# The recurrence of a four-mixer network: kk transposed by 128-token blocks, state sums on the diagonal blocks, 16x16 inverses one block to a lane, and a new order

## The chip, the core and the metric

The kernel is one program on one core of a Trainium2 chip. Five engines run side by side, each in its own order: TensorE (PE; the loading of its stationary operand is listed as PEld), VectorE (DVE), ScalarE (ACT), GpSimd (POOL) and SyncE (SP); the last two mostly start transfers. The metric is device microseconds (us) of one execution; lower is better.

## The reference, cut to what matters

Four mixers, each followed by a feed-forward block, on 512 tokens of width 1024 in float32. The change lies in the first mixer, a gated recurrence over tokens with 16 heads of width 64:

```
def step(state, inp):
    r_t, d_t, k_t, v_t, kk_t, a_t = inp
    sa = jnp.einsum('bhvk,bhk->bhv', state, kk_t)
    state = (state * d_t[:, :, None, :]
             - sa[..., None] * (kk_t * a_t)[:, :, None, :]
             + v_t[..., None] * k_t[:, :, None, :])
    return state, jnp.einsum('bhvk,bhk->bhv', state, r_t)
```

The other mixers (windowed attention, a gated chunk mixer, gated linear attention) and the feed-forward blocks are not touched, but the order of their instructions is.

## The kernel before

**A program that orders itself.** The code first records every operation (line 253 is where each of them is issued, so nearly all rows of the profile carry L253 and are told apart by tile and shape). `Program.run` then picks, engine by engine, which recorded operation goes next, from prices written in the code and from a turn: the operation's own number, shifted by the table `TURNS`, whose entries (first, last, shift) move a range of operations forward or back. When TensorE would have nothing to do for long, or too little in the last window, it is given products of the identity with itself into a spare bank (line 520, `products`): these are the fills.

**The recurrence in chunks.** The 16 heads are worked in four groups of four (two pairs of heads, i = 0, 1, each pair in 128 rows, the second head h in the upper 64). The 512 tokens are four blocks of 128 (b), each of two chunks of 64 (c). For a group, `ahead(n)` runs these, in this order:

- `rwkv_prepare`: decays, keys and the scaled vectors. Tile `qk` of a pair holds for each block four pieces of 64 columns, r, kk, kk, r (outer pieces r, inner pieces kk); `kb` holds the keys likewise.
- `rwkv_products`: for each 128 columns and each head one product of `kb` with `qk`, masked on VectorE into tile `pr` (odd groups) or `pa` (even groups). It holds for each unit (block, pair, head) the triangular matrices that couple the tokens of a chunk.
- `rwkv_inverse`: the 64x64 triangular matrices are inverted, beginning with their 16x16 diagonal blocks. These are gathered into a tile of 128x512 (`et`) whose second half of each 32 columns is zero, transposed in 32x32 squares on VectorE, and inverted by substitution in 15 steps (one product and one sum each, two blocks to a lane); another transpose, a mask (`mt`), and two levels of 64x64 products on TensorE build the whole inverse (`iv`).
- `rwkv_direct`: kk is transposed on TensorE (128 columns of `qk` at a time, so that each transpose carries one piece of r that nobody uses) and multiplied with the inverse; the result goes back into the inner pieces of `qk`.

Then `rwkv_chain` goes through the eight chunks one after another. A step takes the state `st` (128x256, for each pair two 64x64 blocks on the diagonal of a 128x128 square, the rest kept at zero), adds its product with `qk` to the chunk's values (bank `x`), copies that to `vu`, sums `tok` transposed times `vu` onto the old state in bank `pb`, and scales the sum by the chunk's decay (`pend`) into the next state. `rwkv_out` normalizes and gates the result.

While the chain of group n runs, `ahead(n + 1)` is worked beside it; the first group is worked beside the product that makes the values, and the last chain beside the output product over the first three groups (`rwkv_out_proj`, tiles `et` and `rk`). So VectorE, ScalarE and TensorE each mix instructions of a chain with those of the next group.

## Time and profile before

| what | value |
|---|---|
| median of 3 runs | 2467.82 us (2465.43 to 2470.07) |
| the profiled execution | 2470.02 us |
| its span, first to last instruction | 2468.3 us |
| TensorE clock granted, mean | 0.997 of full speed |

On a profile's rows: a group of instructions is written as line, engine, operation, output <- inputs (tile names without numbers), shapes, xcount, then busy us and mean ns of one, then the idle time just before them and who ended it. A matmul of float32 leaves two records or more, a transpose one. The busy us of a group count overlapping instructions once; the mean of one is its own duration, so on TensorE the mean is longer than the spacing. A line of a window gives, for a stretch from:to, its length, the busy us of each engine with its instructions in brackets, the granted clock, the share of the transfer engines and GB/s.

### The profile page before, as it was taken

What the parts mean: (1) busy time and instruction counts of PE and PEld (TensorE: products, weight loads), DVE (VectorE), ACT (ScalarE), POOL (GpSimd) and SP (SyncE); (2) the same over time, 40 slices, a digit from 0 to 9 for tenths busy, and PEclk for the clock granted to TensorE, in tenths of its full rate; (3) what the DMA queues carried; (4) which work ended last, traced back from release to release, by engine and by line L of the source; (5) the groups of instructions that cost most, each with busy time, mean ns of one, the idle gap of its engine ahead of it and who ended that gap; (6) DMA issues with size and microseconds to landing.
All of it is one profiled execution on the core that took longest, in us unless ns stands there. A gap on an engine that the chain in (4) does not pass through costs nothing.

```text
span 2468.3 us, 37524 instructions
## 1 busy us (share of the span) xinstructions
PE 2411.1 (98%) x14166; PEld 1995.9 (81%) x14166; DVE 1930.5 (78%) x3051; ACT 1389.3 (56%) x2267; POOL 400.2 (16%) x456
## 2 busy tenths in 40 slices
PE   9999999999999999999999999999999999999998
PEld 7677789987888768988887788887878788888886
DVE  8686995786779885777789886976868978886868
ACT  4545544664646476656466544854546756755555
POOL 0000000111112241121111300211111221212111
PEclk9999999999999999999999999999999999999999
DMA  5220002589898234898988835889897775989885
GB/s 170 71 71 10 11 11 81 137 226 215 208 221 187 75 107 103 192 238 192 233 189 202 218 99 153 183 201 216 200 225 182 187 181 124 187 214 227 216 211 125
DMA packets 128629, 400.85 MB, mean 162 GB/s; under 512 B 14384, under 2 KB 21040, under 8 KB 128448
## 3 DMA queue, kind: packets, MB, share of 16 engines
q0 software_dynamic: 50688, 171.99, 39.2%
q1 hardware_dynamic: 77760, 226.47, 27.2%
q8 instruction: 111, 1.82, 0.3%
q14 instruction: 70, 0.57, 0.1%
HBM read 393.95 MB, written 2.10 MB: 160 GB/s over the span
## 4 chain that ended last, share of the span: by engine, by line
PE 71%; DMA 9%; DVE 9%; ACT 5%; issue 4%; POOL 1%; SPq 0%; DVEq 0%; POOLq 0%; ACTq 0%
PE ps L253 71%; DMA wraw<-ffn_w_a 3%; DMA wraw<-ffn_w_b 2%; DVE wlo L253 2%; ACT slot L253 2%; DVE slot L253 2%; DMA wraw<-ffn_o_a 2%; ACT whi L253 1%; DVE h L253 1%; POOL wraw L253 1%; DVE et L253 1%; DMA wraw<-sg_w_v 1%; DVE mt L253 0%; DMA wraw<-gla_w_qk 0%; POOL slot L253 0%
## 5 line engine op out<-in xcount | busy, mean ns | idle before, releaser
L253 PE MATMUL ps<-whi,slot 128*128 128x512 f32 (+1 forms) x4960 | 1509.7, 385 | 13.7 <-DVE slot L253 7.4
L253 PEld LDWEIGHTS ps<-whi,slot 128*128 128x128 f32 x4960 | 923.4, 188 | 186.2 <-DVE slot L253 14.7
L253 ACT CAST whi<-wraw 128x1024 fp32r<-128x1024 f32 (+2 forms) x680 | 673.8, 997 | 619.5 <-PE ps L253 426.6
L253 DVE TENSOR_TENSOR wlo<-wraw,whi 128x1024 fp32r<-128x1024 f32 (+2 forms) x680 | 783.7, 1161 | 237.9 <-ACT whi L253 233.8
L253 PE MATMUL ps<-wlo,slot 128*128 128x512 f32 (+1 forms) x2480 | 932.7, 383 | 4.1 <-DVE wlo L253 4.1
L253 PEld LDWEIGHTS ps<-wlo,slot 128*128 128x128 f32 x2480 | 466.8, 188 | 85.7 <-DVE wlo L253 7.9
L253 PE MATMUL ps<-slot,whi 128*128 128x512 f32 (+3 forms) x976 | 276.1, 366 | 1.8 <-ACT slot L253 0.9
L253 DVE TENSOR_TENSOR slot<-ps,slot 128x512 f32<-128x512 f32 (+2 forms) x269 | 159.0, 607 | 79.7 <-PE ps L253 70.6
L253 PEld LDWEIGHTS ps<-slot,whi 128*128 128x128 f32 (+2 forms) x976 | 170.4, 184 | 40.4 <-issue 4.5
L253 POOL DMA_DIRECT2D wraw<-ffn_w_a x128 | 111.0, 879 | 483.2 <-DVE wlo L253 339.4
L253 DVE TENSOR_TENSOR h<-h,ps 128x512 f32<-128x512 f32 x240 | 159.0, 684 | 26.6 <-PE ps L253 24.3
L253 DVE TENSOR_TENSOR slot<-left,slot 128x512 fp32r<-128x512 f32 x250 | 160.2, 662 | 23.5 <-ACT slot L253 15.4
L253 PE MATMUL ps<-slot,wlo 128*128 128x512 f32 (+3 forms) x488 | 176.5, 366 | 0.0
L253 ACT CAST slot<-left 128x512 fp32r<-128x512 f32 (+1 forms) x250 | 143.4, 601 | 29.0 <-PE ps L253 18.0
L253 ACT COPY slot<-ps 128x512 f32<-128x512 f32 (+2 forms) x154 | 85.3, 566 | 72.4 <-PE ps L253 66.0
L253 PEld LDWEIGHTS ps<-slot,wlo 128*128 128x128 f32 (+2 forms) x488 | 89.5, 184 | 18.4 <-issue 3.7
L253 POOL DMA_DIRECT2D wraw<-ffn_o_a x64 | 55.9, 873 | 297.3 <-DVE wlo L253 210.5
L253 POOL DMA_DIRECT2D wraw<-ffn_w_b x64 | 55.1, 867 | 300.2 <-DVE wlo L253 99.4
L253 PE MATMUL ps<-ident,slot 128*128 128x128 f32 (+2 forms) x672 | 88.8, 265 | 6.6 <-DVE slot L253 6.4
L253 PEld LDWEIGHTS ps<-ident,slot 128*128 128x128 f32 (+2 forms) x672 | 68.8, 140 | 31.1 <-DVE slot L253 10.6
L253 DVE TENSOR_TENSOR slot<-slot 128x512 fp32r<-128x512 f32 (+7 forms) x131 | 77.2, 611 | 12.1 <-DMA slot<-slot 7.2
L253 ACT COPY left<-ps 128x512 f32<-128x512 f32 x100 | 51.0, 555 | 44.1 <-PE ps L253 44.0
(281 smaller groups left out, 2242.0 us busy)
## 6 DMA issues: line engine op xcount, KB each, us to landing
wraw<-ffn_w_a SPq DMA_DIRECT2D x128, 512.0 KB, 6.4
wraw<-ffn_w_a POOLq DMA_DIRECT2D x128, 512.0 KB, 7.9
wraw<-ffn_o_a SPq DMA_DIRECT2D x64, 512.0 KB, 5.1
wraw<-ffn_o_a POOLq DMA_DIRECT2D x64, 512.0 KB, 7.1
wraw<-ffn_w_b SPq DMA_DIRECT2D x64, 384.0 KB, 4.0
wraw<-ffn_w_b POOLq DMA_DIRECT2D x64, 384.0 KB, 6.6
wraw<-ffn_o_b SPq DMA_DIRECT2D x16, 512.0 KB, 3.9
wraw<-ffn_o_b POOLq DMA_DIRECT2D x16, 512.0 KB, 7.3
```

The source lines that it names most:

```text
L253: op = self.add(eng.name, lambda: getattr(eng.target, what)(*map(real, args), **{k: real(a) for k, a in kw.items()}), *self.price(eng.name ...
```

## The change

- **kk by blocks of 128 tokens.** The two inner pieces of `qk` change places (chunk 0's kk stands at piece 2, chunk 1's at piece 1), so the two middle pieces of a block, 128 columns, are just the two chunks' kk. One transpose takes them both: four for a pair where there were eight, and one copy where there were two. Writing the pieces in the new places takes two products and two small copies on VectorE for one of each. In `rwkv_products` the right operand picks its two pieces with a step.
- **16x16 inverses, a block to a lane.** ScalarE gathers the diagonal blocks into the full 128x512 tile (no zeros); after the transpose one select takes for each lane the half that is its own; the substitution goes two rows at a time on 256 columns, with a one-column update in between; ScalarE copies the result into both halves before the second transpose, and the mask is applied in two parts. The mask's last column is inverted (`odd` becomes `even`), and the identity that is loaded for it is 256 wide.
- **State sums on the diagonal blocks.** In `rwkv_chain` the product of `tok` and `vu` is made for each head alone, 64x64 outputs into the two halves of the rows, and from the second chunk on the scaling is one product over the whole 128x256 tile.
- **`TURNS`** is written anew: finer ranges, other shifts, for all stages.

```diff
 TURNS = (
-    (0, 192, -3283), (192, 384, -2134), (384, 412, -1837), (412, 464, -482), (464, 492, -1382), (536, 588, -2292), (616, 644, 25), (696, 724, -1506),
...
-    (16911, 17104, -1), (17104, 17297, -15), (17297, 17490, 81), (17490, 17683, -5), (17683, 17876, 295), (17876, 18069, 278), (18069, 18262, 2577),
+    (0, 96, -1837), (96, 192, -1135), (192, 288, -902), (288, 384, -841), (384, 412, 180), (464, 492, 721), (492, 508, 1201), (536, 588, 116),
...
+    (17847, 17948, 1984), (17948, 18048, 2039), (18048, 18149, 3494), (18149, 18250, 9031),
 )
...
+            mid = lambda t, c: t.rearrange("p (b x c) -> p b x c", b=NB, x=4)[:, :, 2 - c, :]
...
-            nc.vector.tensor_mul(inner(qk)[:, :, :, 1:], nat(kk)[:, :, :, 1:], nat(e)[:, :, :, :C - 1])
-            nc.vector.tensor_copy(inner(qk)[:, :, :, 0], nat(kk)[:, :, :, 0])
+            for c in range(2):
+                nc.vector.tensor_mul(mid(qk, c)[:, :, 1:], nat(kk)[:, :, c, 1:], nat(e)[:, :, c, :C - 1])
+                nc.vector.tensor_copy(mid(qk, c)[:, :, 0], nat(kk)[:, :, c, 0])
...
-                    nc.tensor.matmul(ps[h][:, c * P:(c + 1) * P], sb['kb'][i][q, t], sb['qk'][i][q, t], start=c == 0, stop=True, skip_group_check=True)
+                    qk = sb['qk'][i].rearrange("p (b x c) -> p b x c", b=NB, x=4)[q, hf * 2 + c // 2, c % 2:c % 2 + 3:2, :]
+                    nc.tensor.matmul(ps[h][:, c * P:(c + 1) * P], sb['kb'][i][q, t], qk, start=c == 0, stop=True, skip_group_check=True)
...
-        nc.gpsimd.memset(zx4[:, :, 1, :], 0.0)
+        zx, n, tt = [self.part("et") for _ in range(3)]
+        nc.sync.dma_start(tt[:, :256], self.d['rw_eye'])
...
-            nc.vector.scalar_tensor_tensor(zx4[r, :, 0, :], z3[r, o + 16:o + 32, :], mk['odd'][r], z3[r, o:o + 16, :],
-                                           op0=ALU.mult, op1=ALU.add)
+            nc.scalar.copy(zx[r].rearrange("p (t x u) -> p x t u", t=16, x=2), zc[r, o:o + 32, :].rearrange("p (x t) u -> p x t u", x=2))
         nc.vector.transpose(n, zx)
-        for i in range(1, 16):
-            w = tmp[:, :2 * i * i].rearrange("p (b j m) -> p b j m", b=2, j=i)
-            nc.vector.tensor_mul(w, n4[:, i, :, :i].unsqueeze(2).to_broadcast([P, 2, i, i]), t4[:, :, :i, :i])
-            nc.vector.tensor_reduce(t4[:, :, :i, i], w, axis=AX.X, op=ALU.add)
-        tx = self.part("et")
-        nc.vector.transpose(tx, tt)
+        nc.vector.scalar_tensor_tensor(n3, nb[:, :, 0, :], mk['even'], nb[:, :, 1, :], op0=ALU.mult, op1=ALU.add)
+        for i in range(0, 16, 2):
+            if i:
+                w = n[:, :2 * i * i].rearrange("p (c j m) -> p c j m", c=2, j=i)
+                nc.vector.tensor_mul(w, n3[:, i:i + 2, :i].unsqueeze(2).to_broadcast([P, 2, i, i]), t3[:, :i, :i].unsqueeze(1).to_broadcast([P, 2, i, i]))
+                nc.vector.tensor_reduce(t3[:, :i, i:i + 2].rearrange("p j c -> p c j"), w, axis=AX.X, op=ALU.add)
+            nc.vector.scalar_tensor_tensor(t3[:, :i + 1, i + 1], t3[:, :i + 1, i], n3[:, i + 1, i:i + 1], t3[:, :i + 1, i + 1], op0=ALU.mult, op1=ALU.add)
+        nc.scalar.copy(zx.rearrange("p (j b i) -> p j b i", j=16, b=2), t3.unsqueeze(2).to_broadcast([P, 16, 2, 16]))
+        nc.vector.transpose(n, zx)
...
-            src = tu[:, k * 8:k * 8 + 8, :].unsqueeze(2).to_broadcast([P, 8, 4, 16])
-            nc.vector.tensor_mul(t0.rearrange("p (u b j) -> p u b j", u=8, b=4), src, b16)
+            for g in range(2):
+                nc.vector.tensor_mul(t0.rearrange("p (u g x j) -> p g u x j", u=8, g=2, x=2)[:, g], tu[:, k * 8:k * 8 + 8], b16[:, g].unsqueeze(1).to_broadcast([P, 8, 2, 16]))
...
+            kt, tp = self.part("mt"), self.bank()
+            for b in range(NB):
+                nc.tensor.transpose(tp[:, b * P:(b + 1) * P], sb['qk'][i][:, b * 256 + 64:b * 256 + 192], self.ident)
+            nc.scalar.copy(kt, tp)
             for bb in range(2):
-                kt, tp = self.part("mt"), self.bank()
-                for j in range(4):
-                    t = (bb * 4 + j) * P
-                    nc.tensor.transpose(tp[:, j * P:(j + 1) * P], sb['qk'][i][:, t:t + P], self.ident)
-                nc.scalar.copy(kt, tp)
...
-                    for i in range(G):
-                        mm(pb[:, col(i)], tok[:, col(c * 2 + i)], vu[:, col(i)], start=st is None and i == 0, stop=True)
+                    for i, h in heads:
+                        mm(pb[h * 64:(h + 1) * 64, hc(i, h)], tok[:, c * W:(c + 1) * W][:, hc(i, h)], vu[:, hc(i, h)], start=st is None and i == 0, stop=True)
...
-                    for h in range(2):
-                        pend = sb['pend'][h * 64:(h + 1) * 64, :, 2 * b + c].unsqueeze(2).to_broadcast([64, G, 64])
-                        nc.vector.tensor_mul(block(ns, h), block(pb, h), pend)
+                    if st is None:
...
+                    else:
+                        two = lambda t: t.rearrange("p (g c) -> p g c", g=G)
+                        nc.vector.tensor_mul(two(ns), two(pb), sb['pend'][:, :, 2 * b + c].unsqueeze(2).to_broadcast([P, G, P]))
```

More of the change, by code (lines that the diff above doesn't have):

```diff
@@ L1115, in rwkv @@
         m = lambda j: mk[:, j * 64:(j + 1) * 64]
-        self.mk = dict(prod=mk[:, :2 * P], low=(m(4), m(5)), b16=m(6), odd=mk[:, 7 * 64:])
+        self.mk = dict(prod=mk[:, :2 * P], low=(m(4), m(5)), b16=m(6), even=mk[:, 7 * 64:])
         ka1 = cp.tile([P, KT], F32, name="ka1")
@@ L1292, in rwkv_inverse @@
-        tx = self.part("et")
-        nc.vector.transpose(tx, tt)
-        tu = tx.rearrange("p (j u) -> p u j", j=16)
-        b16 = mk['b16'].rearrange("p (b j) -> p b j", b=4).unsqueeze(1).to_broadcast([P, 8, 4, 16])
+        nb = n.rearrange("p (t b m) -> p t b m", t=16, b=2)
+        n3, t3 = [t[:, :256].rearrange("p (a b) -> p a b", a=16) for t in (zx, tt)]
+        nc.vector.scalar_tensor_tensor(n3, nb[:, :, 0, :], mk['even'], nb[:, :, 1, :], op0=ALU.mult, op1=ALU.add)
[5 more added lines that the diff above has]
+            nc.vector.scalar_tensor_tensor(t3[:, :i + 1, i + 1], t3[:, :i + 1, i], n3[:, i + 1, i:i + 1], t3[:, :i + 1, i + 1], op0=ALU.mult, op1=ALU.add)
@@ L1912, in consts @@
     low = [(s6 // (2 * m) == c // (2 * m)) & (s6 % (2 * m) >= m) & (c % (2 * m) < m) for m in (16, 32)]
-    masks = [even, odd] + low + [s6 // 16 == c // 16, (s % 32 >= 16)]
+    masks = [even, odd] + low + [s6 // 16 == c // 16, (s % 32 < 16)]
     masks = np.concatenate([m.astype(np.float32) for m in masks], axis=1)
-    f = np.arange(S)
-    eye = np.broadcast_to((f // 32 == f % 16).astype(np.float32), (P, S)).copy()
+    f = np.arange(256)
+    eye = np.broadcast_to((f // 16 == f % 16).astype(np.float32), (P, 256)).copy()
     return {'rw_masks': masks, 'rw_eye': eye, 'rope_freq': freq}
```

14 lines of the change are left out of this document (7 added, 7 removed), and 40 rows, old and new, of the table TURNS.

## The prediction, made before the changed kernel had run

> **What bounds the kernel now.** The profiled execution took 2470.0 us, 1.7 more than its span, and lies 2.2 above the median of the runs. I read the page first, then busy time in stretches, then the chain of waits in the recurrence, then single instructions.
>
> ```profile
> span 2468.3 us, 37524 instructions
> PE 2411.1 (98%) x14166; PEld 1995.9 (81%) x14166; DVE 1930.5 (78%) x3051; ACT 1389.3 (56%) x2267; POOL 400.2 (16%) x456
> ```
>
> TensorE has work nearly everywhere, so what leaves TensorE shortens the run, and what leaves VectorE does so only where TensorE waits for it. Busy time by stage, with everything first and the filling products (line 520) second:
>
> ```profile
> core 0: us, PE busy (x) PEld busy (x) DVE busy (x) ACT busy (x) POOL busy (x), PEclk, DMA share, GB/s
> 175.00:250.00 75.00, 72.75 (x912) 56.08 (x911) 52.20 (x118) 37.84 (x73) 2.92 (x6) 1.00 0.03 9
> 250.00:395.00 145.00, 138.36 (x2287) 115.16 (x2288) 123.46 (x289) 70.06 (x154) 7.80 (x13) 1.00 0.08 24
> 395.00:460.00 65.00, 64.98 (x618) 61.23 (x610) 37.16 (x99) 25.34 (x53) 1.91 (x2) 1.00 0.39 120
> ```
> ```profile
> 250.00:395.00 145.00, 6.20 (x44) 5.38 (x44) 1.00 0.08 24
> 395.00:460.00 65.00, 4.56 (x38) 4.48 (x38) 1.00 0.39 120
> ```
>
> Stage 1 (175 to 250: value product, first group, its chain) and stage 3 (395 to 460: last chain beside the output product) are full of TensorE. In stage 2 TensorE idles 145 − 138.4 = 6.6 us and fills 6.2: a slack of 12.8 in which it waits for others. Which others, the chain of waits for stage 2 says, by line and then in pieces:
>
> ```profile
> by line: PE ps L253 45.5%; DVE et L253 12.5%; DVE mt L253 6.7%; DVE out L253 3.5%; issue 3.3%; DVE pa L253 3.0%; DVE h L253 2.5%; DVE pr L253 2.5%; DVE qk L253 1.8%; DVE iv L253 1.8%; ACT L253 1.8%; DVE st L253 1.7%; DVE gmean L253 1.4%; AC
> ```
> ```profile
> 285.88 0.65 DVE et L253
> 286.54 0.65 DVE et L253
> 287.21 0.66 DVE et L253
> 287.88 0.68 DVE et L253
> ```
> ```profile
> PE ps L253 <- DVE st L253: 2.4, 3, 1.1
> ```
>
> TensorE carries 45.5% of 145, 66 us. The listed VectorE items sum to 37.4%; with the cut-off tail I take 40%, 58 us (estimate). The four pieces are the gather of a group's diagonal blocks, standing on the path. VectorE, busy 123.5 of 145, is the second bound, although the longest of TensorE's own waits in stage 2 (last line: the state, us in total, times, longest) is small.
>
> **Part 1, kk transposed at once.** Per group 16 transposes become 8 and four 128x512 copies on ScalarE become two.
>
> ```profile
> L253 PE MATMUL ps<-ident,qk 128*128 128x128 f32 x64 | 11.0, 284 | 0.0
> L253 ACT COPY tok<-ps 128x512 f32<-128x512 f32 x16 | 9.5, 591 | 5.7 <-PE ps L253 5.4
> L253 PE MATMUL ps<-qk 64*128 64x128 f32 x128 | 10.0, 281 | 0.7 <-DVE qk L253 0.7
> L253 DVE TENSOR_TENSOR qk<-et 128x504 f32<-128x504 f32 x4 | 2.7, 678 | 0.4 <-ACT et L253 0.4
> L253 DVE COPY qk<-et 128x8 f32<-128x8 f32 x4 | 0.7, 167 | 0.0
> ```
>
> A transpose takes 11.0 / 64 = 0.17 us of TensorE; 32 fewer are 5.5 us, a quarter (1.4) in stage 1 and the rest (4.1) in stage 2. ScalarE loses 8 x 0.59 = 4.7. The products' right operand now skips one 64-column block; counts and widths are the same. I take zero: the odd groups' products are the third line, 10.0 us, so all four groups' take 20, and a tenth more would be 2. On VectorE one product and one small copy (last lines) become two of each for each of a group's two pairs of heads; at 0.42 for a product of half the width (a row of part 2), 2 x 0.42 − 0.68 + 0.17 = 0.33, 0.7 per group.
>
> **Part 2, the state sum on its diagonal blocks.** A step's two full products (four records) become four 128x64 ones on 64 columns (eight records), into alternate halves of the output partitions. Nearest pieces, one after another, start us and length first:
>
> ```profile
> 353.44 0.68 PE L253 MATMUL ps<-wu,iv 64*64 64x64 f32 x16
> 354.05 0.71 PE L253 MATMUL ps<-st,ident 128*128 128x128 f32 x4
> 355.67 0.71 PE L253 MATMUL ps<-vu,tok 128*128 128x128 f32 x4
> 356.31 0.68 PE L253 MATMUL ps<-vu,pa 128*64 128x64 f32 x8
> 356.92 0.33 PE L253 MATMUL ps<-ident,qk 128*128 128x128 f32 x1
> ```
>
> Start to start the old form takes 356.31 − 355.67 = 0.64 us. Eight records of the new shape, all into one half, take 356.92 − 356.31 = 0.61 (vu,pa); alternating halves, 16 smaller records take 354.05 − 353.44 = 0.61, so eight take 0.31 (wu,iv). The new cost lies between 0.31 and 0.61; I take 0.34, near the alternating row, as the outputs alternate: 0.30 saved a step (0.03 at worst). The Trainium skill, in TensorEngine Tiling (Array Packing), section Key Properties, says that tiles of the array run independently but a change of tiling mode drains it. The alternating row agrees with the first half; by that the step saves the 0.30, and without it 0.03.
>
> ```profile
> L253 PE MATMUL ps<-vu,tok 128*128 128x128 f32 x112 | 19.2, 294 | 1.4 <-ACT vu L253 0.9
> 175.00:250.00 75.00, 4.69 (x28) 1.00 0.03 9
> 250.00:395.00 145.00, 10.43 (x62) 1.00 0.08 24
> 395.00:460.00 65.00, 4.14 (x24) 1.00 0.39 120
> ```
>
> 112 records are 28 steps; by stage (second to fourth line) 7, 15 and 6: 2.1, 4.5 and 1.8 us. The state itself:
>
> ```profile
> L253 DVE TENSOR_TENSOR st<-ps,pend 64x128 f32<-64x128 f32 x56 | 16.1, 287 | 16.0 <-PE ps L253 15.4
> L253 DVE TENSOR_TENSOR h<-ps,h 128x256 f32<-128x256 f32 x16 | 6.2, 420 | 3.4 <-PE ps L253 3.3
> ```
>
> Two half products (16.1 / 28 = 0.58) become one 128x256 at 0.42, except in each chain's first step: 24 x 0.16 = 3.8, some 13 of them (2.1) in stage 2. Off the diagonal the sum stays zero, since the state there was cleared and is only multiplied.
>
> **Part 3, the 16x16 inverses.** Four 32-partition gathers move from VectorE to four 32x512 copies on ScalarE, one 128x256 select follows the transpose, 15 pairs of product and sum become seven pairs on the even sizes with eight one-column updates, and ScalarE widens the result (128x512) before the second transpose.
>
> ```profile
> L253 DVE SCALAR_TENSOR_TENSOR et<-pr,mk 32x256 f32<-32x256 f32 x8 | 5.2, 655 | 0.1
> L253 DVE TENSOR_TENSOR et<-et 128x2 f32<-128x2 f32 (+14 forms) x15 | 4.9, 328 | 0.3
> L253 DVE TENSOR_REDUCE et<-et 128x2 f32<-128x2 f32 (+14 forms) x15 | 4.8, 323 | 0.3
> L253 DVE TENSOR_TENSOR et<-et 128x8 f32<-128x8 f32 x3 | 0.5, 168 | 0.0
> L253 DVE TENSOR_TENSOR et<-et 128x392 f32<-128x392 f32 x3 | 1.7, 554 | 0.0
> L253 DVE SCALAR_TENSOR_TENSOR grs<-rs_t,grs 128x8 f32<-128x8 f32 x24 | 4.3, 180 | 0.4
> L253 ACT COPY et<-kkrs 128x512 f32<-128x512 f32 x6 | 3.7, 628 | 0.0
> ```
>
> From 8 to 392 elements a product grows 386 ns: 1.0 ns an element over 0.16 us. The seven kept sizes (2 x i x i for i = 2 to 14) hold 1120 elements: 7 x 0.16 + 1.12 = 2.2 us, and as much for the sums. So 4.9 + 4.8 − 4.4 = 5.3 goes, with 4 x 0.655 = 2.6; eight updates at 0.18 (1.4) and a select at 0.42 come. Splitting the two 128x512 masks into four of half width adds two starts of 0.16 (0.3). With the 0.7 of part 1 VectorE is relieved of 7.9 − 2.8 = 5.1 us a group. In stage 2 fall the second half of group 1's inverse and all of groups 2 and 3: 2.4 x 5.1 = 12.2. ScalarE gains 5 x 0.63 − 2 x 0.59 = 2.0 a group, hidden in its 75 idle us of stage 2; without that cover 8 us in all. No row has the strided gather on ScalarE: at best 0.63 each, at worst twice that, as the 32x256 gather on VectorE costs 655 against 420 for a plain 256-wide one. I take 0.7: 2.8 in series, against 2.6 now. The transposes now wait for ScalarE twice, and behind the first of them stand state products and masks of the running chain; a copy that is late by one other copy costs 0.6, eight times 4.8 at worst, and the order puts other VectorE work ahead. The constant's load on SP's queue halves and is done early; the fill of zeros on GpSimd goes.
>
> **Part 4, places.** All turns are new, up to the last stage. After 460 TensorE waits thus:
>
> ```profile
> 460.00:2468.30 2008.30, 1964.48 (x9542) 1633.59 (x9540) 1585.04 (x2306) 1166.25 (x1850) 384.89 (x422) 1.00 0.77 184
> PE ps L253 <- DVE slot L253: 20.1, 15, 3.5
> 600.00:625.00 25.00, 21.50 (x91) 17.30 (x90) 12.58 (x14) 11.60 (x15) 2.59 (x3) 0.93 0.78 189
> ```
>
> Of 43.8 idle us, 20.1 in 15 waits stand behind VectorE. The work there is unchanged, so I take zero, bounded by half of that row, 10 us, either way.
>
> **Sum.** Stage 1: 1.4 + 2.1 = 3.5. Stage 2 by capacity: 4.1 + 4.5 = 8.6, and half of the slack of 12.8, 15.0; by the chain: 58 x (12.2 + 2.1) / 123.5 + 66 x 8.6 / 132.2 (busy less fills) = 6.7 + 4.3 = 11.0. I take 13.0, the middle. Stage 3: 1.8. Together 18.3: 2470.0 becomes 2451.7, and the median 2467.8 becomes **2449.5**.
>
> **Rivals.** *A, VectorE hides:* only TensorE's work counts, the slack stays, and part of it is filled again: 5.5 + 8.4 = 13.9 less two waits of the longest kind after 460 (3.5 each), 2461. For it: TensorE named only 2.4 us of waits for the state. Against it: the chain stands on VectorE for 58 us. *B, more:* all slack of stage 2 goes (3.5 + 21.4 + 1.8 = 26.7) and the places win up to 10: 2431 to 2441. For it: 20.1 us in 15 waits behind VectorE are there to be moved. *C, slower:* in the feed-forward stages a weight load or its adding load is put later in SP's or GpSimd's queue, and TensorE waits as at 600 to 625: 3.5 idle and 0.07 x 25 of clock, 5.3 a gap. Four gaps cancel the forecast; from five it is slower by more than noise, 6 give 2467.8 − 18.3 + 31.8 = 2481. For it: the transfers' share there is 0.78; against: TensorE's long waits there name VectorE. *D, the clock:* with less TensorE work the recurrence is granted less; at a mean of 0.75 over the 132.2 − 8.6 = 123.6 us of work left in stage 2 it costs 41, 2490. In every stage's row the clock stands at 1.00, even with 6.6 idle. The Trainium skill, in TensorE: Matmul & The Clock Gate, Part 1, has the clock halved after a window of some 3.4 us without matmuls; the row of 600 to 625 agrees, and none of the recurrence comes near. *E, it does not do what it says:* the new products do not overlap (0.03 x 28 = 0.8) and the gathers take 1.26 each, 2.4 a group later, 7 over three groups, which eats VectorE's relief: 2467.8 − 6.3 + 3 = 2465.
>
> **Chances.** Forecast 0.48 (2444 to 2456), A 0.20, B 0.18, C 0.07, D 0.03, E 0.04. The range 2433 to 2464 holds forecast, A and two thirds of B; left out are the rest of B, C, D and most of E, under 0.2. No change means within 0.2% (4.9 us), what a measurement of this kernel can tell: faster 0.48 + 0.18 + 0.18 of A = 0.84, same 0.02 + 0.04 = 0.06, slower 0.10.
>
> **What would show it.** Part 1: 32 fewer transposes and eight fewer 128x512 copies. Part 2: tok records 128x64, twice as many, under 0.4 us a step, and 24 state products of 128x256 near 0.42. Part 3: seven pairs a group, gathers on ScalarE near 0.7. Sum: the output product's start comes 15 to 17 us earlier, VectorE's busy time falls by about 4 x 5.1 + 3.8 = 24, and after 460 idle stays near 44. I am wrong if stage 2 keeps its length with more fill, or if the time after the recurrence moves by more than 10.

## The result, and the profile after

The changed kernel takes 2469.52 us (median of 12 executions, 2462.29 to 2475.57), the kernel before in the same comparison 2469.55 (12, 2462.62 to 2473.57): a ratio of 1.0004, 95% interval 0.9991 to 1.0016. Nothing was gained where 18.3 us were forecast. The profiled execution took 2467.0. Page of the changed kernel, span and busy time by engine:

```profile
span 2465.3 us, 37624 instructions
PE 2399.4 (97%) x14222; PEld 1985.7 (81%) x14222; DVE 1909.0 (77%) x3007; ACT 1408.0 (57%) x2282; POOL 404.4 (16%) x452
```

The work did leave its engines: TensorE 11.7 us less, VectorE 21.5 less (24 were forecast), ScalarE 18.7 more. So the question is where the time went. Busy time by stage, as before the change, everything first and the fills second (now line 530; L253 has become L263):

```profile
175.00:250.00 75.00, 70.84 (x936) 55.84 (x935) 44.94 (x114) 37.96 (x71) 2.33 (x4) 0.95 0.03 9
250.00:395.00 145.00, 136.13 (x2406) 113.52 (x2406) 114.06 (x283) 86.85 (x181) 8.43 (x12) 0.99 0.10 32
395.00:460.00 65.00, 65.00 (x580) 60.84 (x580) 37.01 (x83) 27.64 (x62) 1.90 (x2) 1.00 0.37 116
```
```profile
175.00:250.00 75.00, 3.37 (x18) 2.63 (x19) 0.95 0.03 9
250.00:395.00 145.00, 0.46 (x4) 0.26 (x3) 0.99 0.10 32
```

The fills of stage 2 are nearly gone (6.2 to 0.5), so the order found other products to do. But TensorE idles 8.9 us there where it idled 6.6, and 4.2 in stage 1 where it idled 2.3, and its clock, 1.00 in both stages before, is 0.95 and 0.99. The chain of waits of stage 2 and TensorE's waits over the recurrence say who makes it wait:

```profile
by line: PE ps L263 60.2%; ACT et L263 7.9%; DVE mt L263 3.9%; DVE pa L263 3.4%; DVE h L263 3.2%; issue 3.1%; DVE et L263 2.8%; DVE pr L263 2.5%; ACT out L263 1.8%; DVE ew L263 1.6%; ACT mt L263 1.5%; ACT L263 1.5%; DVE iv L263 1.3%; ACT vu
```
```profile
PE ps L263 <- ACT vu L263: 6.7, 5, 2.9
PE ps L263 <- ACT out L263: 2.2, 1, 2.2
```

VectorE's `et` has fallen from 12.5% to 2.8% of the path, as meant. In its place stands ScalarE's `et`, 7.9% of 145 = 11.5 us, which was too small before to be in the part of the list that is shown. Of these, 7.7 us are the gathers of two groups (the chain's pieces at 279.8 to 284.2 and 340.8 to 345.1 us); the others are other copies into `et`. And TensorE, which waited once for a `vu` before (0.9 us, in the row of `tok` quoted above), waits five times, 6.7 us. The groups that answer to those of the prediction:

```profile
L263 PE MATMUL ps<-vu,tok 128*64 128x64 f32 x224 | 13.5, 241 | 5.9 <-ACT vu L263 5.7
L263 PE MATMUL ps<-ident,qk 128*128 128x128 f32 x48 | 8.4, 296 | 0.0
L263 DVE TENSOR_TENSOR st<-ps,pend 128x256 f32<-128x256 f32 x24 | 10.1, 420 | 15.1 <-PE ps L263 14.9
L263 ACT COPY et<-pr 32x512 f32<-32x512 f32 x8 | 8.6, 1069 | 0.2
L263 ACT COPY et<-et 128x512 f32<-128x512 f32 x3 | 1.9, 619 | 0.1
L263 DVE STREAM_TRANSPOSE et<-et 128x512 f32<-128x512 f32 x6 | 4.3, 709 | 10.9 <-ACT et L263 10.9
```

A gather copy takes 1.07 us on ScalarE, where 0.7 was taken. Here is the second group's row of four in the timeline of ScalarE, then of TensorE at the same time (start us, length; in brackets the idle time before, and who ended it):

```profile
229.54 1.07 ACT L263 COPY mt<-ps 128x512 f32<-128x512 f32 x2 [2.53 <-PE ps L263]
230.50 4.29 ACT L263 COPY et<-pr 32x512 f32<-32x512 f32 x4
234.82 0.37 ACT L263 COPY vu<-ps 64x256 f32<-64x256 f32 x1
```
```profile
230.22 0.61 PE L263 MATMUL ps<-st,h 128*128 128x128 f32 x4
231.63 0.68 PE L263 MATMUL ps<-wu,iv 64*64 64x64 f32 x16
235.23 0.70 PE L263 MATMUL ps<-vu,tok 128*64 128x64 f32 x8 [2.92 <-ACT vu L263]
235.72 1.06 PE L263 MATMUL ps<-vu,pa 128*64 128x64 f32 x8
```

The bank that `vu` is copied from is ready at 230.83, when the product of the state with `qk` ends (`st,h`: in this group `qk` lies in a tile named `h`). The copy starts at 234.82, 4.0 us later, without any idle time before it: ScalarE was never free. TensorE has other products until 232.31 and then stands idle. Behind this copy stand the chain's state sum and everything after it. The products that follow take longer, too (`vu,pa` 1.06 us, 0.68 in the row quoted before the change), since the clock has dropped: it is 0.51 from 235 to 242 us. The two ends of the recurrence, the first product with the value weights and the second output product, for before and after:

```profile
20.12 2.24 PE L253 MATMUL ps<-slot,whi 128*128 128x512 f32 x8 [0.92 <-ACT slot L253]
```
```profile
L253 PE MATMUL ps<-whi,rk x32: 388/394/482, 456.9 to 470.1; 128*128 128x512 f32 x32
```
```profile
18.88 2.25 PE L263 MATMUL ps<-slot,whi 128*128 128x512 f32 x8 [0.92 <-ACT slot L263]
```
```profile
L263 PE MATMUL ps<-whi,rk x32: 388/394/482, 447.0 to 460.2; 128*128 128x512 f32 x32
```

Between them lie 456.9 − 20.1 = 436.8 us before and 447.0 − 18.9 = 428.1 after. I call this the length of the recurrence below: it fell by 8.7, not by 18.3. The rest was lost later: from 447.0 to the end are 2018.3 us, from 456.9 to the end 2011.4 before. TensorE in the later stages:

```profile
460.00:2465.30 2005.30, 1955.30 (x9491) 1625.24 (x9489) 1580.26 (x2296) 1159.93 (x1829) 389.45 (x422) 1.00 0.77 184
```

It idles 50.0 us, 6.2 more than before, in stages whose work did not change.

### The profile page after: what moved, and what is told of

It is laid out like the page before. It is cut to its first block, busy times and chain, and to the rows that moved or that the text cites. A ratio compares the mean times of both kernels' runs of the same rounds, so it can differ in the third digit from the quotient of the medians.

```text
span 2465.3 us, 37624 instructions
## 1 busy us (share of the span) xinstructions
PE 2399.4 (97%) x14222; PEld 1985.7 (81%) x14222; DVE 1909.0 (77%) x3007; ACT 1408.0 (57%) x2282; POOL 404.4 (16%) x452
## 4 chain that ended last, share of the span: by engine, by line
PE 68%; DVE 10%; DMA 9%; ACT 5%; issue 5%; POOL 1%; SPq 0%; DVEq 0%; POOLq 0%; ACTq 0%
PE ps L263 68%; DMA wraw<-ffn_w_a 4%; DVE wlo L263 3%; DVE slot L263 3%; DMA wraw<-ffn_w_b 2%; DVE h L263 2%; ACT slot L263 2%; DMA wraw<-ffn_o_a 1%; ACT whi L263 1%; POOL wraw L263 1%; ACT et L263 1%; DMA wraw<-sg_w_v 0%; DMA wraw<-ffn_o_b 0%; DVE mx L263 0%; SPq L263 0%
## 5 line engine op out<-in xcount | busy, mean ns | idle before, releaser
L263 PE MATMUL ps<-whi,slot 128*128 128x512 f32 (+1 forms) x4960 | 1514.2, 384 | 14.0 <-DVE slot L263 8.6
L263 PEld LDWEIGHTS ps<-whi,slot 128*128 128x128 f32 x4960 | 921.2, 188 | 191.0 <-issue 11.4
L263 ACT CAST whi<-wraw 128x1024 fp32r<-128x1024 f32 (+2 forms) x680 | 672.8, 996 | 616.4 <-PE ps L263 408.6
L263 DVE TENSOR_TENSOR wlo<-wraw,whi 128x1024 fp32r<-128x1024 f32 (+2 forms) x680 | 782.2, 1159 | 276.7 <-ACT whi L263 273.4
L263 PE MATMUL ps<-wlo,slot 128*128 128x512 f32 (+1 forms) x2480 | 933.6, 382 | 5.6 <-DVE wlo L263 5.5
L263 PEld LDWEIGHTS ps<-wlo,slot 128*128 128x128 f32 x2480 | 465.9, 188 | 85.6 <-DVE wlo L263 9.5
L263 PE MATMUL ps<-slot,whi 128*128 128x512 f32 (+3 forms) x976 | 284.5, 368 | 2.9 <-DVE slot L263 1.8
L263 DVE TENSOR_TENSOR slot<-ps,slot 128x512 f32<-128x512 f32 (+2 forms) x269 | 158.1, 605 | 64.6 <-PE ps L263 52.2
L263 PEld LDWEIGHTS ps<-slot,whi 128*128 128x128 f32 (+2 forms) x976 | 171.8, 185 | 42.3 <-issue 4.6
L263 POOL DMA_DIRECT2D wraw<-ffn_w_a x128 | 110.7, 869 | 491.8 <-DVE wlo L263 319.0
L263 PE MATMUL ps<-slot,wlo 128*128 128x512 f32 (+3 forms) x488 | 177.9, 365 | 1.0 <-DVE wlo L263 1.0
L263 DVE TENSOR_TENSOR slot<-left,slot 128x512 fp32r<-128x512 f32 x250 | 160.3, 661 | 23.3 <-ACT slot L263 18.0
L263 DVE TENSOR_TENSOR h<-h,ps 128x512 f32<-128x512 f32 x240 | 158.7, 682 | 18.0 <-PE ps L263 16.2
L263 ACT CAST slot<-left 128x512 fp32r<-128x512 f32 x250 | 143.4, 602 | 42.8 <-PE ps L263 25.0
L263 ACT COPY slot<-ps 128x512 f32<-128x512 f32 (+1 forms) x152 | 83.9, 566 | 60.8 <-PE ps L263 57.6
L263 POOL DMA_DIRECT2D wraw<-ffn_o_a x64 | 55.3, 865 | 325.6 <-DVE wlo L263 168.5
L263 PEld LDWEIGHTS ps<-slot,wlo 128*128 128x128 f32 (+2 forms) x488 | 90.3, 185 | 19.0 <-issue 2.6
L263 POOL DMA_DIRECT2D wraw<-ffn_w_b x64 | 55.4, 883 | 291.4 <-DMA wraw<-ffn_w_b 125.3
L263 PE MATMUL ps<-ident,slot 128*128 128x128 f32 (+1 forms) x672 | 90.0, 264 | 7.8 <-DVE slot L263 3.6
L263 PEld LDWEIGHTS ps<-ident,slot 128*128 128x128 f32 (+1 forms) x672 | 69.6, 139 | 31.4 <-DVE slot L263 8.0
L263 DVE TENSOR_TENSOR slot<-slot 128x512 fp32r<-128x512 f32 (+6 forms) x123 | 74.2, 623 | 11.8 <-ACT slot L263 5.4
L263 DVE SCALAR_TENSOR_TENSOR slot<-slot,ncol 128x512 f32<-128x512 f32 (+1 forms) x96 | 65.3, 701 | 8.0 <-ACT slot L263 7.6
```

The costliest lines, as they stand in the source:

```text
L263: op = self.add(eng.name, lambda: getattr(eng.target, what)(*map(real, args), **{k: real(a) for k, a in kw.items()}), *self.price(eng.name ...
```

## The experiments

Unless said otherwise, a ratio is to the kernel before on the same chip, with its 95% interval. "Old places" are the shifts of the kernel before, moved by the twelve operations that the change saves in the recurrence.

**Recurrence and places apart.** First the old places behind the changed recurrence, then the new places behind the old recurrence.

```diff
 TURNS = (
...
-    (4306, 4405, 88), (4405, 4504, 260), (4504, 4603, -219),
+    (4801, 4999, 304), (4999, 5197, 198), (5197, 5395, 70),
```

> The changed recurrence with its new turns, but all operations after the first mixer with the turns of the kernel before. Theory (the recurrence gains about 9 us and the new places after it lose about 7): 7 to 10 us faster than before. Rival (the later stages of the one profiled execution were chance, the recurrence gains nothing in the mean): within 3 us of before.

> The kernel before with its recurrence untouched and the new turns only for the operations after the first mixer. Theory: 5 to 9 us slower than before, the loss between 800 and 1400 us of the span (windowed attention to the chunk mixer). Rival (chance): within 3 us of before.

Measured: 2461.29 us, 0.9977 [0.9967, 0.9987], and 2476.32 us, 1.0031 [1.0019, 1.0044]. So the recurrence with its new places gains 5.7 us, less than the 7 to 10 that were expected, and the new places behind it lose 7.6. Part 4 of the change, costed at nothing, eats the gain.

**The gather's step on the other side.** The copies read in order and write with a step; no other instruction changes.

```diff
-            nc.scalar.copy(zx[r].rearrange("p (t x u) -> p x t u", t=16, x=2), zc[r, o:o + 32, :].rearrange("p (x t) u -> p x t u", x=2))
+            nc.scalar.copy(zx[r].rearrange("p (t x u) -> p x u t", t=16, x=2), zc[r, o:o + 32, :].rearrange("p (x t) u -> p x u t", x=2))
```

> The changed kernel in the same order of instructions; only the four gather copies of each inverse walk pr along its contiguous 16 elements and write with a step, where they read with a step of 1 KB. Theory (the gather stands on the path and starves TensorE): a gather copy falls from 1.07 to about 0.65 us, TensorE's waits of 2.9 and 1.8 us behind it go below 1, the half-clock windows at 235 to 242 and 286 to 289 us go, and the time falls 4 to 8 us below the kernel before. Rival 1 (it is the write or the 32 partitions, not the reading step, that costs): copies stay at 1.07, no change. Rival 2 (ScalarE is hidden, the gain went elsewhere): copies are shorter but the time stays within 2 us.

> The changed recurrence with contiguous gathers and the turns of before after the first mixer. Theory: the two effects add, 12 to 17 us faster than before. Rival (either effect is chance or they overlap): no faster than the better of the two alone.

> The same base (2456.65 us), every instruction in the same order, with the gathers reading in order and writing with the step, as in the first experiment (no gain there) and in the run that added it to the old places (2461.29 to 2460.21). Both theories: 2453 to 2458, no difference from the base that can be measured; a fall of 5 us or more would mean that the reading step matters to something else than the copy's own length.

Alone: 2469.68 us, 1.0008 [0.9998, 1.0017]; the copies still take 1.06 to 1.14 us, which is rival 1. With the old places as well: 2460.21, 0.9967 [0.9955, 0.9979]; on the base of the best places (below, 0.9953) 2452.56, 0.9935 [0.9923, 0.9948]. In none of the three is there a difference from its base that the intervals tell apart. It does not matter which side has the step.

**Each part alone, and the places alone.** One part of the change in the kernel before, every operation at its old place; then all three parts at the old places; then the new places without any part.

```diff
+            for c in range(2):
+                nc.vector.tensor_mul(mid(qk, c)[:, :, 1:], nat(kk)[:, :, c, 1:], nat(e)[:, :, c, :C - 1])
...
+                    for i, h in heads:
+                        mm(pb[h * 64:(h + 1) * 64, hc(i, h)], tok[:, c * W:(c + 1) * W][:, hc(i, h)], vu[:, hc(i, h)], start=st is None and i == 0, stop=True)
...
+            nc.scalar.copy(zx[r].rearrange("p (t x u) -> p x t u", t=16, x=2), zc[r, o:o + 32, :].rearrange("p (x t) u -> p x t u", x=2))
```

> The kernel before with part 1 alone (kk of a 128-token block transposed at once), every operation keeping the turn that it had. The sum had 5.5 us of TensorE for it and 0.7 a group more of VectorE. Theory (TensorE's work in the recurrence counts in full): 4 to 6 us faster. Rival (the chain of waits in the recurrence runs over others, the room becomes idle time or fills): within 2 us, with the fills or idle between 250 and 395 us up by about 4.

> The kernel before with part 2 alone (state sums on the diagonal blocks). The sum had 8.4 us of TensorE and 3.8 of VectorE. Theory: a step's sum takes about 0.3 us and the time falls by 6 to 10. Rival 1 (no overlap): 0.6 a step, time within 2. Rival 2 (chain latency is not on the path): records as short as hoped, time falls under 4.

> The kernel before with part 3 alone (inverses a block to a lane, gathered by ScalarE). The sum gave it about 5 us a group of VectorE. Theory (gather copies of 1.07 us in a row hold the chain's copies and eat what VectorE gains): within 3 us of before or slower, half-clock windows appear in the recurrence that before has not. Rival (VectorE's relief counts): 3 to 7 us faster.

> All three parts of the change together, each operation at the place it had in the kernel before (new operations at that of the work they replace); no new place anywhere. Theory (a list of places fits one exact list of operations, and the parts together save engine time that only a fitted order turns into a shorter span): slower than before by 5 to 20 us, 2473 to 2488, as each part alone was (15 to 20 us). Rival (the parts help each other, and the new places only moved things about): 2455 to 2468, the recurrence shorter by 5 us or more.

> The kernel before, none of the three parts in it, with the changed kernel's places for the operations of the recurrence that both have, and its own old places from there on. Theory (places fit one list of operations): slower than before by 5 to 25 us, 2473 to 2493, with more idle time of TensorE between 250 and 395 us. Rival (the gain of 5.7 us in the recurrence came of the new places, not of the parts): 2460 to 2465, the recurrence shorter by about 5 us without any part.

Measured: transposes alone 2483.16 us, 1.0061 [1.0039, 1.0082]; state sums alone 2486.68, 1.0079 [1.0060, 1.0097]; inverses alone 2487.98, 1.0086 [1.0069, 1.0102]; all three at the old places 2498.42, 1.0128 [1.0112, 1.0145]; the new places on the old work 2525.41, 1.0239 [1.0225, 1.0253]. Each part takes work away and yet each makes the kernel 15 to 20 us slower. The fills of stage 2, with the transposes alone:

```profile
250.00:395.00 145.00, 12.70 (x80) 10.21 (x80) 1.00 0.06 17
```

They were 6.2 us before: room that this part left was filled again, as I read it because nothing was placed to come forward. A part's worth can't be read from the part alone here: a table of shifts fits one list of operations, and each of these five mixtures of lists and places was ordered worse. The two mixed runs were worse than their ranges said. One thing fits the theory of the third run: of the three parts only the inverses lower the clock of stage 2 (0.96; 1.00 with either of the others), and there TensorE waits 5.3 us for `vu` (2.0 and 2.7). But an experiment that is to tell something must keep every instruction's place.

**Two tries at the gathers that did change the order.** Two of a group's four copies made on VectorE; and the program's own price for such a copy set to what the trace shows (both with the old places behind the recurrence, 0.9977).

```diff
+            gather = nc.scalar.copy if k % 2 else nc.vector.tensor_copy
+            gather(zx[r].rearrange("p (t x u) -> p x t u", t=16, x=2), zc[r, o:o + 32, :].rearrange("p (x t) u -> p x t u", x=2))
...
+        if eng == "ACT" and what == "copy" and n == 512 and views[0].shape[0] == 32:
+            return 1060.0, 250.0
```

> The changed recurrence with the old places behind it, as in the run of the old places after the recurrence (2461.29 us), and of each group's four gather copies the first and the third are made on VectorE, the second and the fourth on ScalarE. Theory (four gathers of 1.07 us in a row on ScalarE hold the chain's own copies in its queue, TensorE stands idle some 3 us behind them and its clock is halved in the next windows): the row on ScalarE falls to about 2.1 us, TensorE's idle time in front of the matrix that takes the held copy shrinks by about 2 us a group, the half-clock windows in the recurrence go or shrink, and the time falls by 3 to 6 us to 2455 to 2459. Rival (the recurrence's length is set by the order as a whole and the gathers' hold is only where the slack shows): VectorE's two more copies of about 0.6 us a group and the shifted order give back what ScalarE's queue gains, 2459 to 2466.

> As the run of the old places after the recurrence (2461.29 us), but the program's own price for a 32x512 copy on ScalarE is 1060 ns, which is what the trace shows, in place of about 520 ns; no instruction changes, only the order that the program works out from its prices. Theory (the stall at the gathers comes of an order that counts on copies half as long): with the true price the program fills TensorE's wait behind the gathers with other matrices, the idle time of 1.8 to 3 us at each group shrinks, and the time falls by 2 to 5 us to 2456 to 2459. Rival (the places of the recurrence were fitted to the wrong price, and any other order loses): 2463 to 2475.

Measured 2464.73 us, 0.9986 [0.9976, 0.9997], and 2470.76, 1.0013 [1.0003, 1.0024]. Both theories of a gain failed, by the numbers of the rivals. In both profiles the clock of stages 1 and 2 is back at 1.00, but the recurrence is 431.7 and 436.3 us long (450.8 − 19.1 and 455.8 − 19.5, between the same two ends), against 449.5 − 19.7 = 429.8 in the base. This doesn't clear the gathers, since the order moved with the edit.

**The gathers alone, and VectorE alone, every place kept.** The program goes on ordering by the old shapes, and the instruction that is issued is cut down. The first of these two kernels leaves out most of the gathering, the second most of VectorE's arithmetic in the inverses, so neither computes what the reference does.

```diff
+            if k == 0:
+                Program.cut = lambda a, p=iter((zx, z[:, :512])): next(p).real()
+            else:
+                Program.cut = lambda a: a[:, :1, :1]
             nc.scalar.copy(zx[r].rearrange("p (t x u) -> p x t u", t=16, x=2), zc[r, o:o + 32, :].rearrange("p (x t) u -> p x t u", x=2))
...
```

> The changed recurrence with the old places behind it (2461.29 us before this run, ratio 0.9977), every instruction in the same order on every engine, but of a group's four gather copies the first is a plain 128x512 copy and the other three copy 32x16 elements, so that the row of four takes about 1.2 us in place of 4.3; the inverses are then not those of the reference. Theory 1 (the gathers' hold of ScalarE's queue is what the recurrence loses): TensorE's idle time behind the held copies shrinks by 2 to 3 us in each of the groups, the half-clock windows of the recurrence go, and the time falls by 6 to 10 us to 2451 to 2455. Theory 2 (the recurrence is as long as TensorE's own work in it plus what the order leaves, so that a shorter copy only moves the wait): 2458 to 2462.

```diff
...
+                Program.cut = lambda a: a[:, :1, :1]
                 nc.vector.tensor_mul(w, n3[:, i:i + 2, :i].unsqueeze(2).to_broadcast([P, 2, i, i]), t3[:, :i, :i].unsqueeze(1).to_broadcast([P, 2, i, i]))
...
```

> As the run of the old places behind the recurrence, every instruction in the same order, but VectorE's part of the 16x16 inverses is cut once more: the seven pairs of product and sum work on one element, the select on four, the second transpose on 32 columns, about 3.1 us a group less (7 us of it between 250 and 395 us), so the inverses are not those of the reference. Theory of the prediction (VectorE's relief shortens the recurrence, 0.47 us for each us by the chain of waits, half of it by the capacity): the time falls by 3 to 5 us to 2456 to 2458. Rival A of the prediction (VectorE's relief hides, only TensorE's work counts): 2460 to 2463.

Measured: gathers cut 2450.98 us, 0.9922 [0.9906, 0.9939]; VectorE cut 2461.30, 0.9979 [0.9968, 0.9990], against 0.9977 for the base. The first is theory 1, at its strong end; the second is the prediction's rival A. Windows of stages 1 and 2, gathers cut, then VectorE cut:

```profile
175.00:250.00 75.00, 71.84 (x976) 56.30 (x976) 48.53 (x118) 37.57 (x76) 3.75 (x6) 1.00 0.03 9
250.00:395.00 145.00, 141.84 (x2464) 119.92 (x2461) 116.77 (x300) 82.16 (x182) 7.04 (x10) 1.00 0.11 34
```
```profile
175.00:250.00 75.00, 70.84 (x932) 55.62 (x932) 40.60 (x114) 37.01 (x70) 2.33 (x4) 0.95 0.03 9
250.00:395.00 145.00, 136.09 (x2406) 113.69 (x2405) 107.72 (x283) 86.80 (x179) 8.44 (x12) 0.99 0.10 32
```

With VectorE cut its busy time is 4.3 and 6.3 us below the changed kernel's in the two stages, and TensorE's figures and its clock don't move. With the gathers cut TensorE idles 3.2 us in stage 2 (8.9 in the changed kernel) and its clock stays at 1.00. The recurrence, between the two ends above, is then 437.1 − 19.5 = 417.6 us long, 19.2 shorter than before the change:

```profile
19.53 2.25 PE L256 MATMUL ps<-slot,whi 128*128 128x512 f32 x8 [0.92 <-ACT slot L256]
```
```profile
L256 PE MATMUL ps<-whi,rk x32: 388/394/477, 437.1 to 450.3; 128*128 128x512 f32 x32
```

**Where the later places lose.** Old places in windowed attention alone; then from the end of the recurrence to the second feed-forward block (447 to about 1290 us); then only from there to the end.

```diff
 TURNS = (
-    (4306, 4405, 88), (4405, 4504, 260), (4504, 4603, -219),
...
-    (10073, 10173, 42),
+    (4801, 4999, 304), (4999, 5197, 198), (5197, 5395, 70),
...
+    (9973, 10173, 36),
```

> The changed kernel, with the turns of before in the windowed-attention mixer alone (about 780 to 950 us) and the new ones everywhere else. Theory (most of the loss of the new places lies there): 4 to 7 us faster than the changed kernel, so about 5 below before. Rival (the loss is spread over the stages): at most 3 below before.

> The changed kernel with the old places from the end of the recurrence to the end of the second feed-forward block (about 447 to 1290 us), new places elsewhere. Single profiles put 7 to 10 us of the later loss before 1290 us, but with the old places in windowed attention alone nothing came back. Theory (the loss lies in this stretch as a whole): 2460 to 2464, as with all old places. Rival (the loss is spread, or lies behind): 2465 to 2470.

> The changed kernel with the new places up to the end of the second feed-forward block (about 1290 us) and the old places from there on. Theory (the loss lies in the first stretch): 2468 to 2472, nothing comes back. Rival (spread): half comes back, 2464 to 2467; lies behind: 2460 to 2463.

Measured: attention alone 2467.80 us, 1.0002 [0.9989, 1.0016]; first half 2456.65, 0.9953 [0.9934, 0.9971]; second half 2478.24, 1.0036 [1.0022, 1.0049]. With the runs of all old (0.9977) and all new places (1.0004) this makes a square that adds up: in the first half the new places cost 0.0051 and 0.0059 of the time, 13 to 15 us, and in the second they gain 0.0024 and 0.0032, 6 to 8 us. Attention alone gave nothing back, as its rival had it. The first half was below its range and the second above: that the new places gain in the second half had not been thought of. TensorE over the first half, changed kernel and then with old places there (both begin the second output product at 447):

```profile
447.00:1290.00 843.00, 819.52 (x3941) 1.00 0.75 180
```
```profile
PE ps L263 <- DVE slot L263: 12.9, 11, 2.6
PE ps L263 <- ACT slot L263: 4.8, 2, 2.5
PE ps L263 <- ACT whi L263: 2.2, 2, 1.2
```
```profile
447.00:1290.00 843.00, 827.17 (x3996) 1.00 0.75 181
```
```profile
PE ps L256 <- DVE slot L256: 12.7, 9, 3.4
PE ps L256 <- DVE wlo L256: 1.2, 2, 0.6
PE ps L256 <- DVE h L256: 1.1, 1, 1.1
PE ps L256 <- ACT slot L256: 0.5, 2, 0.3
```

TensorE is 7.7 us busier with the old places. The waits for VectorE's `slot`, on which the prediction had its eye, are the same; those for ScalarE fall from 7.0 us to 0.5. That does not make them the cause. The 4.8 us for ScalarE's `slot` lie in windowed attention (at 876 and 916 us); with the old places in attention alone they are 0.4, and the time stayed where it was. The two waits for `whi`, 2.2 us, are for rounded copies of weights that ScalarE could begin only when the weights had arrived:

```profile
483.38 0.83 ACT L263 CAST whi<-wraw 128x768 fp32r<-128x768 f32 x1 [1.86 <-DMA wraw<-ffn_w_b]
1103.64 1.04 ACT L263 CAST whi<-wraw 128x1024 fp32r<-128x1024 f32 x1 [2.85 <-DMA wraw<-ffn_w_a]
```

These are single profiles (the second kernel's is 8 us below its median). What makes up the 13 to 15 us of the first half stays open.

**All the work, with shorter gathers.** On that base every instruction keeps its place; the gathers write the elements in the order in which they read them, in runs of 32, and VectorE's transpose takes them out with the step.

```diff
-            nc.scalar.copy(zx[r].rearrange("p (t x u) -> p x t u", t=16, x=2), zc[r, o:o + 32, :].rearrange("p (x t) u -> p x t u", x=2))
-        nc.vector.transpose(n, zx)
+            nc.scalar.copy(zx[r].rearrange("p (u t) -> p u t", u=16), zc[r, o:o + 32, :].rearrange("p t u -> p u t"))
+        nc.vector.transpose(n.rearrange("p (t x u) -> p t x u", t=16, x=2), zx.rearrange("p (u x t) -> p t x u", u=16, x=2))
```

> The run with the old places from the recurrence's end to the second feed-forward block (2456.65 us, ratio 0.9953), every instruction in the same order, but the gathers on ScalarE write the 512 elements in the order in which they read them (runs of 32), and VectorE's transpose that follows reads them with the step in their place. Theory (the length of the row of four gathers on ScalarE is what the recurrence loses, and VectorE's time hides): the gathers fall from 1.07 to about 0.63 us each, the row from 4.3 to 2.5, and the time by 4 to 7 us to 2450 to 2453, even if the transpose takes 1.4 us in place of 0.7. Rival (a stepped transpose on VectorE is in the same series and gives it back, or the copy from runs of 32 costs as much as before): 2454 to 2459.

Measured 2447.63 us (2444.18 to 2456.62), 0.9919 [0.9904, 0.9934], from 0.9953: faster than both kernels. The fall of 9.0 us is more than the 4 to 7 of the theory, whose price for the copies came true. Against the run beside it on the same chip, which has the same places and the long copies (2452.56 us, 0.9935), it is 4.9, and the two intervals overlap; the recurrence in the profiles tells the two apart better. Groups, windows of stages 1 and 2, TensorE's waits over the recurrence and the two ends:

```profile
L256 ACT COPY et<-pr 32x512 f32<-32x512 f32 x8 | 4.9, 615 | 0.2
L256 DVE STREAM_TRANSPOSE et<-et 128x512 f32<-128x512 f32 x6 | 5.3, 883 | 5.5 <-ACT et L256 5.5
```
```profile
175.00:250.00 75.00, 71.52 (x959) 56.02 (x958) 47.53 (x118) 37.95 (x74) 2.74 (x5) 1.00 0.03 9
250.00:395.00 145.00, 140.36 (x2458) 118.14 (x2457) 117.42 (x293) 84.69 (x184) 8.02 (x12) 1.00 0.11 34
```
```profile
PE ps L256 <- ACT vu L256: 3.3, 5, 1.1
```
```profile
20.21 2.25 PE L256 MATMUL ps<-slot,whi 128*128 128x512 f32 x8 [0.92 <-ACT slot L256]
```
```profile
L256 PE MATMUL ps<-whi,rk x32: 388/394/482, 439.5 to 452.7; 128*128 128x512 f32 x32
```

The same copies take 0.62 us, a row of four 2.5. The three transposes that read with the step take more (a mean of 883 over three that step and three that don't: 2 x 883 − 709 = 1057 ns). TensorE waits 3.3 us for `vu` in place of 6.7. The recurrence is 439.5 − 20.2 = 419.3 us long, 17.5 shorter than before the change, where 18.3 were forecast, and 8.8 shorter than the changed kernel's 428.1.

## Why the prediction was wrong, point by point

**What failed first: the price of the gather, and what waits behind it.** "No row has the strided gather on ScalarE: at best 0.63 each, at worst twice that ... I take 0.7: 2.8 in series". It is 1.07, a row of four 4.3. The bounds held, the value taken was at the wrong end. That alone would be 1.5 us a group, 6 in all. It cost more by the next step: "ScalarE gains ... 2.0 a group, hidden in its 75 idle us of stage 2", and "a copy that is late by one other copy costs 0.6, eight times 4.8 at worst". ScalarE's busy time rose by 18.7 us where 8 were worked out, and it does have idle time on the mean. But four copies stand in its queue in one piece, ahead of a `vu` copy whose bank had been ready for 4.0 us, and the chain stands behind that copy. With copies of 0.62 us and every place kept the recurrence is some 9 us shorter, so this step, put at nothing, cost about that. The prediction named what waits behind the transpose on VectorE, and not what waits behind the gathers on ScalarE. Rival E did price a gather at 1.26, but as a group that is later by 2.4 us and as VectorE's relief lost, not as a hold on the chain's own copies.

**The clock.** Rival D was set at 0.03 because "even with 6.6 idle" the clock had stood at 1.00. A lower clock came, in small: 0.95 over stage 1 and 0.99 over stage 2 are 0.05 x 75 + 0.01 x 145 = 5.2 us. It did not come by D's mechanism, less work for TensorE: with the gathers shortened or cut that work is the same, and the clock is 1.00 in both stages. It came behind the waits. So the hold costs twice, once as a wait and again as a slower clock behind it. Profiles with the same order and copies as long show the two apart. The changed recurrence with the old places behind it, 0.95 and 0.98 in the two stages, loses 6.7 us of clock by the same working, and its recurrence is 429.8 us long. The run with the step on the other side and the old places waits as long for `vu` (6.8 us) but lost little of the clock:

```profile
175.00:250.00 75.00, 69.77 (x949) 54.68 (x948) 46.62 (x116) 39.24 (x73) 2.33 (x4) 1.00 0.03 9
250.00:395.00 145.00, 137.39 (x2418) 114.84 (x2417) 114.40 (x288) 86.23 (x180) 8.24 (x12) 0.99 0.10 32
```

That is 1.5 us, and its recurrence is 445.1 − 19.4 = 425.7 us long. So 5.2 us of clock go with 4.1 of length, and without any loss of clock it would be about 424.5 (an estimate from two profiles). Of the 8.8 us between 428.1 and 419.3 some 3.5 are then the clock and some 5 the wait.

**What failed second: places at zero.** "The work there is unchanged, so I take zero, bounded by half of that row, 10 us, either way." They cost 7.6 us in all, inside the bound, made of some 14 lost up to the second feed-forward block and some 7 gained after it. The bound came from the waits behind VectorE, which stayed as they were in the first half; what the 14 are made of stays open. Rival C had the right sign, and two waits of its kind came, for weights that arrived late, but of 2.2 us together where it had 5.3 for each gap. With some 9 lost in the recurrence and 7.6 in the places, 1.7 of the 18.3 are left (an estimate from profiles and medians), which the result can't tell from nothing.

**What held.** The `tok` step takes 0.28 us (0.34 taken): in the timeline eight records start at 285.20 and the next product at 285.48.

```profile
285.20 0.45 PE L263 MATMUL ps<-vu,tok 128*64 128x64 f32 x8 [1.77 <-ACT vu L263]
285.48 0.63 PE L263 MATMUL ps<-vu,pr 128*64 128x64 f32 x8
```

The scaling takes 420 ns on 128x256, as taken, in 24 instances. A transpose stays at 8.4 / 48 = 0.17. VectorE is relieved by 21.5 us where 24 were worked out. And with gathers of 0.62 the recurrence is 17.5 us shorter, near the sum of 18.3 with the price that it assumed. That is the total alone; how far its terms are right is the next point.

**What stays open.** The sum paid VectorE's relief by halves of two readings. The run with VectorE cut shows that while the gathers hold ScalarE more relief buys nothing. What the relief is worth with short gathers was not tried, so the chain reading's 6.7 us are neither shown nor refuted. That rival A's 2461 is the time of the changed recurrence under old places is chance: A had the slack stay because VectorE's relief hides, and the slack went as soon as ScalarE let go.

**"I am wrong if stage 2 keeps its length with more fill, or if the time after the recurrence moves by more than 10."** Neither came true in these words: there was less fill, and the later time moved by 7. A test of the reading should also have named idle time with less fill, which is what came.

## What to carry to other kernels

Before work is moved to an engine that has idle time on the mean, look at which instruction of the critical chain will queue behind it there, and price the whole piece of work that stands ahead in one row, at the price of its access pattern. Where a table of places is fitted to a list of operations, judge neither a part of a change nor a new table by itself: keep every instruction's place and change only what one of them costs.

## What had not been expected of the hardware

A copy of 512 float32 on 32 partitions takes 1.07 us on ScalarE when the elements step singly on either side, and 0.62 when both sides run over 32 neighbours, as long as the widening copy of 128x512 that runs over 16 (0.62 in the groups of the changed kernel): 0.45 us, or 0.88 ns for each element. On VectorE the step costs a transpose 1057 − 709 = 348 ns, 0.68 ns an element. The Trainium skill, Vector Engine (DVE) Microarchitecture Reference, section 5.2 Measured stream behaviour on trn2, says that a port keeps its full rate only while neighbouring pairs of words are read or written, and that single hops cost about 0.65 cycle an element, more where the step is small. By the 0.96 GHz that it gives there this is 0.68 ns (an estimate), and the transpose here, with a step of 32 words, agrees; no smaller step was tried. These figures are for VectorE; the 0.88 ns measured on ScalarE are more.

The clock fell after a single wait. TensorE's wait in the rows above was 2.92 us, and the 25 us around it have a mean of 0.86, which is 7 us at half speed:

```profile
225.00:250.00 25.00, 22.02 (x191) 17.10 (x191) 16.84 (x53) 13.65 (x22) 0.00 (x0) 0.86 0.00 1
```

After the wait of 1.77 us that ends at 285.20 the clock is 0.66 from 285 to 290 us. But in the run with the step on the other side and the old places the same wait, 2.88 us there, is followed by a clock of 1.00 from 235 to 242 us. The Trainium skill, TensorE: Matmul & The Clock Gate, Part 1, has the clock at half after an idle window of about 3.4 us. The 7 us fit two such windows at half speed, but both waits before a fall were shorter than one. What decides whether such a wait lowers the clock no run here shows.
